# Regrouping the sixteen pairs of a Strassen-type product: four groups of four, with a split first group

## The chip, the cores and the metric

The kernel runs on one core of one Trainium2 chip. The metric is the device time of one execution, in microseconds (us). A core has TensorE (PE in the profile, PEld for its weight loads), VectorE (DVE), ScalarE (ACT), GpSimd (POOL) and SyncE (SP), whose queue issues all the DMA transfers of the part that is changed here.

## The reference

One layer of a streaming encoder on x of shape 1024 x 1024, in float32: a token-mixer sub-layer and then a channel mixer. Only the second half of the channel mixer is touched:

```
h2 = modulate(rms_norm(x, g_pre_mlp), sh2, sc2)
f  = square(relu(h2 @ w_mlp_in))            # 1024 x 4096, the first mixer product
ff = f @ w_mlp_out                          # 4096 -> 1024, the second mixer product
x  = x + gt2 * rms_norm(ff, g_post_mlp)
```

## The kernel before

**Precision.** Every float32 operand is split into a high and a low fp32r part (`split`: a ScalarE cast, line 104, and a VectorE subtraction, line 91), and each product is three matmuls: high by high, high by low, low by high.

**The second mixer product.** The 4096 summed rows are 16 pairs of 128-row slices. For a group of pairs the 2x2 block product is done in seven multiplications instead of eight, in the order 1, 2, 6, 5, 7, 3, 4 (`ORDER`, `STEPS`). A *step* is one of the seven for one group: for each of four row blocks b, one PSUM bank gets three matmuls of 128x512 from every pair of the group (`product`, line 1379), and then the bank is added into the result `acc` in SBUF (`gather`): by a ScalarE copy the first time a quarter of the result is touched (line 1387), by a VectorE addition otherwise (line 1389). The bank family "a" is kept through steps 1, 6, 7 and 4 of a group, "b" serves step 2, "c" steps 5 and 3. PSUM has eight banks here, all in one pool.

**Factors.** A step's left and right factors are raw rows or sums of raw rows. `load` brings the raw rows by roles A, B, C and D (sides x: `w_mlp_out`, y: the stored activation `f_d`), one 256 KB transfer per role, pair and side. `make(n)` adds or subtracts them as `SUMS` says (line 1288), splits the result into `factor_at` tiles, and starts loads for the next group. Pairs 0 and 1 of a group have their raw rows in `g` tiles, pairs 2 and 3 in `h` tiles; the role X (first written in step 2) lives in `wh` and `wl` tiles, two buffers each, which the first mixer product also uses for its outgoing rows (`fo`, stored to `f_d` by line 1340). Factor tiles alternate between two sets (`n % 2`).

**Groups before.** `GROUPS = (2, 4, 4, 4, 2)`. The first group of two pairs starts inside the tail of the first mixer product (`mlp_tail`). The last group of two goes block by block: for one row block all seven steps, then the next block, so that `finish_half` can begin early. `finish_half(b, q)` squares one half of a result block on ScalarE into a scratch tile with a row sum (line 1429), multiplies the half by a gain on VectorE (1432), and, when both halves of the block are in, forms the reciprocal root (129 on VectorE, 132 on GpSimd), adds the residual in two VectorE instructions (1437) and stores (1440).

**Order.** In this part no order is written out by hand. A planner places the instructions on each engine from its own simulated timeline; the program order is a preference, and a tile that has no free buffer makes its first writer wait until an older tile of its tag is released. What is placed first on an engine then runs first.

Of the kernel before, what the change touches and what calls it, by code (L numbers as in the profile page):

```python
# [16 lines left out]
P = 128  # L17
# [13 lines left out]
def block_kernel(  # L31
# [28 lines left out]
    def nm(s):  # L60
        uid[0] += 1
        return f"{s}_{uid[0]}"
# [982 lines left out]
    def gslot(dtype=F32, shape=(P, HALF)):  # L1045
        return gp.tile(list(shape), dtype, tag="g", name=nm("g"))
# [58 lines left out]
    def hslot(dtype=F32, shape=(P, HALF)):  # L1105
        return tk.tile(list(shape), dtype, tag="h", name=nm("h"), bufs=16)
# [132 lines left out]

    GROUPS = (2, 4, 4, 4, 2)
    NG = len(GROUPS)
    HERE = {
        "x": {"A": (0, 0), "B": (0, 1), "C": (1, 1), "D": (1, 0)},
# [13 lines left out]
    raw_at, made_at, made = {}, {}, {}  # L1259
    steps = [(g, i) for g in range(NG) for i in ORDER]  # L1260

    def raw_of(role, j, side):
        if (role, j, side) not in raw_at:
            if role == "X":
                for q in range(2):
                    t = raw_tile((P, 2, HALF), "wh" if side == "x" else "wl")
                    for r in range(2):
                        raw_at["X", 2 * q + r, side] = t[:, r, :]
            else:
                raw_at[role, j, side] = gslot() if j < 2 else hslot()  # L1270
        return raw_at[role, j, side]

    def load(g, role, sides="xy"):
        p0 = sum(GROUPS[:g])
        for j in range(GROUPS[g]):
            for side in sides:
                a, n = HERE[side][role]
                m = 2 * (p0 + j) + a
                src = f_d[m] if side == "y" else w_mlp_out[m * P : (m + 1) * P, :]
                nc.sync.dma_start(raw_of(role, j, side), src[:, halves[n]])  # L1280

    def make(n):

        g, i = steps[n]
        for j in range(GROUPS[g]):
            for side, o, a, b, op in SUMS.get(i, ()):
                o, a, b = (raw_of(r, j, side) for r in (o, a, b))
                nc.vector.tensor_tensor(o, a, b, op=op)
        made[n] = []
        for j in range(GROUPS[g]):  # L1290
            fs = []
            for side in "xy":
                to = factor_at(n, j, side)
                split(raw_of(WHERE[side][i], j, side), *to)
                fs.append(to)
            made[n].append(fs)
        if g + 1 < NG:
            for sides, role in {
                5: [("xy", "A")], 7: [("xy", "B")], 3: [("x", "D"), ("y", "C")],
                4: [("x", "C"), ("y", "D")],  # L1300
            }.get(i, ()):
                load(g + 1, role, sides)

    def factor_at(n, j, side):
        g, i = steps[n]
        if g == NG - 1:
            if i in (5, 7):
                return made_at[0, j + 2 * (i == 7), side]
            if i == 4:
                return made_at[1, j, side]  # L1310
            new = {1: lambda: frslot(), 2: lambda: hslot(F32R), 6: lambda: hslot(F32R),
                   3: lambda: gslot(F32R)}[i]
            return new(), new()
        at = n % 2, j, side
        if at not in made_at:
            new = frslot if j >= 2 and n % 2 else yslot
            made_at[at] = new(), new()
        return made_at[at]

    with ExitStack() as es:  # L1320
        def rest_of_h():
            order = """
                53a 50a s50a 51a 52a s51a n0 n1 51b 50b s52a s31 s30 52b 53b s53a 73a 72a 70 s33 s53b 60 s50b s52b s32 71 72b 62 73b s51b 63 61 42 s62 41 s63 s60 40a s42 s71 s61 43 40b s40 s70 s73 s43 s72 s41
            """
            for step in order.split():
                second_half(step)

        def mlp_products(p, xop):
            fo = out_pair()

            def done(r, half, ps, kept):

                o = fo[r][:, half, :]
                if kept is None:
                    nc.scalar.copy(o, ps)
                else:
                    nc.vector.tensor_tensor(o, ps, kept, op=ALU.add)
                nc.vector.scalar_tensor_tensor(o, o, 0.0, o, op0=ALU.max, op1=ALU.mult)
                if (r, half) in ((0, 1), (1, 0)):
                    nc.sync.dma_start(f_d[2 * p + r], flat(fo[r]))  # L1340

            return pair_products(psg, 4, xop, yop, keeper(fo), done, p == 0)

        def mlp_tail(i):
            if i == 1:
                for role in "ADBC":
                    load(0, role)
            elif i == 5:
                make(0)
            elif i == 3:  # L1350
                make(1)

        pipeline(
            NP, mlp_factors, mlp_products, first=(mlp_first, mlp_split), tail=mlp_tail,
            early=rest_of_h
        )
# [3 lines left out]
    with ExitStack() as es:  # L1360
# [4 lines left out]
        def frslot():  # L1365
            return fr.tile([P, HALF], F32R, tag="fr", name=nm("fr"))
# [5 lines left out]
            (4, "a", False, 0, 1),  # L1372
        )

        def product(ps, fs, b, start):
            s = slice(b * P, (b + 1) * P)
            for j, ((xh, xl), (yh, yl)) in enumerate(fs):
                for n, (l, r) in enumerate(((yh, xh), (yh, xl), (yl, xh))):
                    nc.tensor.matmul(  # L1379
                        ps, l[:, s], r, start=start and j == 0 and n == 0,  # L1380
                        stop=j == len(fs) - 1 and n == 2, skip_group_check=True,
                    )

        def gather(ps, b, half, n, fresh):
            o = acc[:, half * 4 + b, halves[n]]
            if fresh:
                nc.scalar.copy(o, ps)
            else:
                nc.vector.tensor_tensor(o, ps, o, op=ALU.add)  # L1389

        seen = set()
        last = 7 * (NG - 1)
        for n in range(last):
            if n % 7 == 0:
                banks = {}
            i, bk, start, half, c = STEPS[n % 7]
            for b in range(4):
                if start:
                    banks[bk, b] = bank(psg, "s")
                product(banks[bk, b], made[n], b, start)  # L1400
                gather(banks[bk, b], b, half, c, (half, c) not in seen)
            seen.add((half, c))
            for m in {last - 3: (last - 1, last), last - 2: (last + 1, last + 2),
                      last - 1: range(last + 3, last + 7)}.get(n, (n + 2,)):
                make(m)
        g2r = [gslot() for _ in range(2)]
        for q in range(2):
            nc.sync.dma_start(g2r[q], mod_d[3:4, halves[q]].broadcast_to([P, HALF]))

        gpm = raw_tile()  # L1410
        nc.sync.dma_start(gpm, g_post_mlp.broadcast_to([P, D]))
        for q in range(2):
# [4 lines left out]
        def finish_half(b, q):  # L1417

            n, s = halves[q], slice(b * P, (b + 1) * P)
            if b not in blocks:  # L1420
                xt = [fr.tile([P, HALF], F32, tag="fr", name=nm("xt")) for _ in "01"]
                for h in range(2):
                    nc.sync.dma_start(xt[h], x1_d[s, halves[h]])
                blocks[b] = xt, raw_tile(tag="wl" if b < 4 else "wh"), sums()
                again = False
            else:
                again = True
            (xt, sq, ss), o = blocks[b], acc[:, b, n]
            nc.scalar.activation(
                sq[:, n], o, AF.Square, scale=D**-0.5, accum_out=ss[:, q : q + 1]  # L1430
            )
            nc.vector.tensor_tensor(o, o, g2r[q], op=ALU.mult)
            if again:
                r = rstd_of(ss)
                for h in range(2):
                    o = acc[:, b, halves[h]]
                    nc.vector.scalar_tensor_tensor(
                        xt[h], o, r, xt[h], op0=ALU.mult, op1=ALU.add
                    )
                    nc.sync.dma_start(out[s, halves[h]], xt[h])  # L1440


        WHOLE = {2: (0, 0), 7: (1, 1), 3: (1, 0), 4: (0, 1)}
        for b in range(4):
            banks = {}
            for n7, (i, bk, start, half, n) in enumerate(STEPS):
                if start:
                    banks[bk] = bank(psg, "s")
                product(banks[bk], made[last + n7], b, start)
                gather(banks[bk], b, half, n, False)  # L1450
                if i in WHOLE:
                    half, q = WHOLE[i]
                    finish_half(4 * half + b, q)
    tk_es.close()
    gp_es.close()
    psg_es.close()
# [29 lines left out]
```

## Time and profile before

| what | value |
|---|---|
| time, median of 3 runs | 1444.85 us (1442.78 to 1446.96) |
| the profiled execution, its own time | 1447.72 us |
| its span, first to last instruction | 1446.0 us |
| TensorE busy in the span | 1375.6 us (95%) |
| VectorE busy | 1075.1 us (74%) |
| ScalarE busy | 653.0 us (45%) |
| mean granted TensorE clock | 0.983 |

Times in rows are us from the start of the span. A row of the timeline merges instructions of one kind; "x3" says how many, and square brackets give the idle time ahead of them and what ended it.

### The profile page before, as it was taken

How to read it: one execution, taken by the hardware profiler on the slowest of the kernel's cores; microseconds unless marked ns; L12 is line 12 of the kernel's file. 1: busy time of each engine (PE TensorE's matmuls, PEld its weight loads, DVE VectorE, ACT ScalarE, POOL GpSimd, SP SyncE). 2: the span in 40 equal slices, each digit the busy share in tenths (PEclk: the TensorE clock that was granted, in tenths of full speed). 3: DMA queues.
4: the chain of work that ended last, by engine and by line, in shares of the span. 5: the costliest groups of instructions: out<-in, count | busy, mean ns of one | idle time of the engine just before them, and what ended most of it. 6: DMA issues, size and time to landing. Idle time of an engine off the chain costs nothing.

```text
span 1446.0 us, 17935 instructions
## 1 busy us (share of the span) xinstructions
PE 1375.6 (95%) x6281; PEld 1124.2 (78%) x6281; DVE 1075.1 (74%) x1684; ACT 653.0 (45%) x1317; POOL 95.3 (7%) x187
## 2 busy tenths in 40 slices
PE   5899899999999999989999899999999899999996
PEld 4788777887888888767788688888888688888884
DVE  6727887887876878728626976665645999989998
ACT  5636656665534444324446643332332534334432
POOL 1003112211200000000001000000000000000001
PEclk9899999999999999999999899999999999999999
DMA  8501111111124776758423143332336425151224
GB/s 300 181 15 34 37 40 35 37 37 52 45 87 142 248 260 205 221 202 309 146 99 116 45 146 117 117 116 86 113 123 218 153 80 175 59 171 33 81 80 174
DMA packets 111742, 178.43 MB, mean 123 GB/s; under 512 B 7786, under 2 KB 67230, under 8 KB 111652
## 3 DMA queue, kind: packets, MB, share of 16 engines
q1 hardware_dynamic: 111652, 177.29, 37.0%
q8 instruction: 49, 0.80, 0.2%
q14 instruction: 41, 0.34, 0.1%
HBM read 135.83 MB, written 41.43 MB: 123 GB/s over the span
## 4 chain that ended last, share of the span: by engine, by line
PE 69%; DVE 14%; DMA 7%; issue 4%; ACT 3%; POOL 1%; SPq 0%; DVEq 0%; ACTq 0%; POOLq 0%
PE s L234 24%; PE s L1379 19%; PE mm L546 10%; PE v L508 3%; PE s L903 3%; DVE pt L690 2%; PE s L123 2%; PE s L121 2%; PE s L122 2%; DMA wa<-in_w_ada_dram 2%; PE o L731 2%; DVE a L694 2%; PE tr L720 1%; DVE acc L145 1%; DMA raw<-in_w_in_dram 1%
## 5 line engine op out<-in xcount | busy, mean ns | idle before, releaser
L1379 PE MATMUL s<-y,y 128*128 128x512 f32 x984 | 236.7, 393 | 7.9 <-DVE ffacc L1389 4.3
L1379 PEld LDWEIGHTS s<-y,y 128*128 128x128 f32 x984 | 185.3, 189 | 50.0 <-DVE ffacc L1389 5.8
L546 PE MATMUL mm<-hTh,wh 128*128 128x512 f32 x320 | 129.1, 403 | 0.0
L546 PE MATMUL mm<-hTh,wl 128*128 128x512 f32 x320 | 125.5, 392 | 0.0
L546 PE MATMUL mm<-hTl,wh 128*128 128x512 f32 x320 | 125.5, 392 | 0.0
L104 ACT CAST y<-g 128x512 fp32r<-128x512 f32 x104 | 58.8, 622 | 127.1 <-PE s L1379 100.8
L690 DVE TENSOR_TENSOR_SCAN pt<-pt,dmask 128x128 f32<-128x128 f32 (+3 forms) x64 | 87.1, 1365 | 8.7 <-ACT pt L683 8.2
L1389 DVE TENSOR_TENSOR ffacc<-s,ffacc 128x512 f32<-128x512 f32 x124 | 84.2, 696 | 8.1 <-PE s L1379 8.1
L234 PE MATMUL s<-mTh,g 128*128 128x512 f32 x256 | 86.3, 404 | 3.7 <-ACT mTh L104 3.7
L104 ACT CAST tu<-tr 128x512 fp32r<-128x512 f32 (+2 forms) x112 | 49.1, 439 | 78.2 <-PE tr L720 49.4
L132 POOL TENSOR_TENSOR rstd<-var,mhalf 128x1 f32<-128x1 f32 x32 | 23.2, 726 | 879.7 <-DVE var L129 879.5
L91 DVE TENSOR_TENSOR tu<-tr,tu 128x512 fp32r<-128x512 f32 (+2 forms) x112 | 55.1, 494 | 34.5 <-ACT tu L104 33.4
L234 PE MATMUL s<-mTh,h 128*128 128x512 f32 x240 | 79.8, 396 | 0.0
L1379 PE MATMUL s<-fr,fr 128*128 128x512 f32 x288 | 74.5, 392 | 0.0
L234 PE MATMUL s<-y,h 128*128 128x512 f32 x288 | 71.7, 391 | 0.0
L91 DVE TENSOR_TENSOR y<-g,y 128x512 fp32r<-128x512 f32 x104 | 68.6, 697 | 4.0 <-PE s L1379 2.3
L234 PE MATMUL s<-y,g 128*128 128x512 f32 x288 | 71.5, 391 | 0.0
L546 PEld LDWEIGHTS mm<-hTh,wl 128*128 128x128 f32 x320 | 60.2, 188 | 13.4
L234 PE MATMUL s<-hTh,t 128*128 128x512 f32 x208 | 67.5, 394 | 0.0
L546 PEld LDWEIGHTS mm<-hTl,wh 128*128 128x128 f32 x320 | 60.5, 189 | 8.8
L546 PEld LDWEIGHTS mm<-hTh,wh 128*128 128x128 f32 x320 | 60.4, 189 | 8.8
L731 PE MATMUL o<-tu,vs 128*128 128x256 f32 x320 | 57.0, 297 | 9.6 <-DVE ot L741 5.0
(293 smaller groups left out, 3147.7 us busy)
## 6 DMA issues: line engine op xcount, KB each, us to landing
raw<-in_w_in_dram SPq DMA_DIRECT2D x38, 512.0 KB, 5.2
wa<-in_w_ada_dram SPq DMA_DIRECT2D x32, 512.0 KB, 4.3
raw<-in_w_mlp_in_dram SPq DMA_DIRECT2D x32, 512.0 KB, 3.7
g<-in_w_mlp_out_dram SPq DMA_DIRECT2D x40, 256.0 KB, 3.1
g<-f_d SPq DMA_DIRECT2D x40, 256.0 KB, 2.8
f_d<-wl SPq DMA_DIRECT2D x16, 512.0 KB, 4.7
f_d<-wh SPq DMA_DIRECT2D x16, 512.0 KB, 3.2
h<-in_w_mlp_out_dram SPq DMA_DIRECT2D x24, 256.0 KB
```

The source lines that it names most:

```text
L91: eng.tensor_tensor(o, a, b, op=ALU.subtract)
L104: nc.scalar.copy(hi, src)
L121: nc.tensor.matmul(ps, lh, rh, start=i == 0, stop=False)
L122: nc.tensor.matmul(ps, lh, rl, start=False, stop=False)
L234: nc.tensor.matmul(ps, l, r, start=first and k == 0 and j == 0, stop=k == nk - 1 and j == 2, skip_group_check=True,)
L508: nc.tensor.matmul(vb[b], l, r, start=k == 0 and i == 0, stop=k == KC - 1 and i == 2, skip_group_check=True,)
L546: nc.tensor.matmul(ps, w[a][:, k, :], hT[b][:, k, s], start=k == 0 and i == 0, stop=k == KC - 1 and i == 2, skip_group_check=True,)
L690: nc.vector.tensor_tensor_scan(pt[:, 0:w][:, ::-1], pt[:, 0:w][:, ::-1], dmask[:, T - w : T][:, ::-1], 1.0, ALU.mult, ALU.max,)
L731: nc.tensor.matmul(po[:, : 2 * P], v, part[:, 0:5:4, :] if j and jp == g else part[:, 2 * j + 1 : 2 * j + 3, :], start=jp == 0 and j == 0 ...
L903: nc.tensor.matmul(ps, l[:, k, s], r, start=k == 0 and i == 0, stop=k == 3 and i == 2, skip_group_check=True,)
L1379: nc.tensor.matmul(ps, l[:, s], r, start=start and j == 0 and n == 0, stop=j == len(fs) - 1 and n == 2, skip_group_check=True,)
L1389: nc.vector.tensor_tensor(o, ps, o, op=ALU.add)
```

## The change

The 16 pairs are now four groups of four. The two pairs that the first group used to have are the first half of a group of four: steps 1 and 2 are done with pairs 0 and 1 and not gathered, pairs 2 and 3 are loaded and split, and steps 1 and 2 are completed with them and gathered. There is no special last group: the last two steps (3 and 4) of the last group alternate by row block. The halves of blocks that are whole earlier are finished after steps 6 (blocks 0 to 3, first half) and 7 (blocks 4 to 7, second half) of the last group. The scratch tile of `finish_half` is now a `raw` tile (three buffers) for all eight blocks, where it was `wl` for blocks 0 to 3 and `wh` for 4 to 7 (two buffers each); the residual rows of blocks 0 to 3 are loaded into `g` tiles.

```
-    GROUPS = (2, 4, 4, 4, 2)
+    GROUPS = (4, 4, 4, 4)
...
+    FIRST_TWO, LAST_TWO = (0, 1), (2, 3)
...
             if i == 1:
                 for role in "ADBC":
-                    load(0, role)
+                    load(0, role, js=FIRST_TWO)
             elif i == 5:
-                make(0)
+                make(0, FIRST_TWO)
             elif i == 3:
-                make(1)
+                make(1, FIRST_TWO)
...
+        def step(n, blocks=range(4), js=range(4), last=True):
             i, bk, start, half, c = STEPS[n % 7]
-            for b in range(4):
-                if start:
+            fs = [made[n][j] for j in js]
+            for b in blocks:
+                if start and js[0] == 0:
                     banks[bk, b] = bank(psg, "s")
-                product(banks[bk, b], made[n], b, start)
-                gather(banks[bk, b], b, half, c, (half, c) not in seen)
+                product(banks[bk, b], fs, b, start and js[0] == 0, last)
+                if last:
+                    gather(banks[bk, b], b, half, c, (half, c) not in seen)
...
+        step(0, js=FIRST_TWO, last=False)
+        for role in "ADBC":
+            load(0, role, js=LAST_TWO)
+        step(1, js=FIRST_TWO, last=False)
+        for n in range(2):
+            make(n, LAST_TWO)
+        for n in range(2):
+            step(n, js=LAST_TWO)
+            make(n + 2)
+        NS = 7 * NG
+        for n in range(2, NS - 5):
+            step(n)
+            make(n + 2)
...
-            if b not in blocks:
-                xt = [fr.tile([P, HALF], F32, tag="fr", name=nm("xt")) for _ in "01"]
+            again = b in blocks
+            if not again:
+                xt = [gslot() if b < 4 else fr.tile([P, HALF], F32, tag="fr", name=nm("xt")) for _ in "01"]
...
-                blocks[b] = xt, raw_tile(tag="wl" if b < 4 else "wh"), sums()
+                blocks[b] = xt, raw_tile(), sums()
...
-        WHOLE = {2: (0, 0), 7: (1, 1), 3: (1, 0), 4: (0, 1)}
+        for n in range(NS - 5, NS - 2):
+            step(n)
+            if n + 2 < NS:
+                make(n + 2)
+            if n == NS - 5:
+                for b in range(4):
+                    finish_half(b, 0)
+            if n == NS - 3:
+                for b in range(4):
+                    finish_half(4 + b, 1)
         for b in range(4):
-            banks = {}
-            for n7, (i, bk, start, half, n) in enumerate(STEPS):
-                ...
+            step(NS - 2, (b,))
+            finish_half(4 + b, 0)
+            step(NS - 1, (b,))
+            finish_half(b, 1)
```

The branch of `factor_at` that gave the last group of two its own factor tiles is gone.

## Rows read from the trace of the kernel before

**Rows 1.** The page's first part: busy time, share of the span, instructions.
```profile
PE 1375.6 (95%) x6281; PEld 1124.2 (78%) x6281; DVE 1075.1 (74%) x1684; ACT 653.0 (45%) x1317; POOL 95.3 (7%) x187
```
**Rows 2.** Windows of the second product: length, busy time (count) by engine, PE clock, DMA.
```profile
1133.60:1137.10 3.50, 1.73 (x6) 0.86 (x5) 3.50 (x7) 2.59 (x6) 0.00 (x0) 1.00 0.37 150
1137.10:1149.30 12.20, 12.10 (x45) 9.51 (x45) 12.20 (x22) 6.12 (x12) 0.00 (x0) 0.86 0.36 108
1149.30:1151.60 2.30, 0.00 (x0) 0.00 (x0) 2.30 (x5) 0.18 (x1) 0.00 (x0) 1.00 0.40 128
...
1230.00:1390.00 160.00, 160.00 (x702) 131.46 (x701) 150.49 (x250) 67.68 (x126) 0.00 (x0) 1.00 0.25 79
...
1415.00:1428.00 13.00, 11.59 (x51) 9.22 (x50) 12.80 (x25) 5.39 (x17) 1.93 (x3) 1.00 0.70 242
1428.00:1436.20 8.20, 4.97 (x18) 3.14 (x18) 8.20 (x17) 1.89 (x5) 2.00 (x3) 1.00 0.49 180
1436.20:1446.00 9.80, 0.00 (x0) 0.00 (x0) 6.22 (x12) 1.01 (x4) 1.59 (x2) 0.76 0.43 161
```
**Rows 3.** Groups by line and shape, 1122.1 us to the end, VectorE.
```profile
L1389 DVE TENSOR_TENSOR ffacc<-s,ffacc 128x512 f32<-128x512 f32 x124 | 84.2, 696 | 8.1 <-PE s L1379 8.1
```
**Rows 4.** Timeline of all engines, 1100 to 1180 us.
```profile
1111.14 5.60 PE L1379 MATMUL s<-y,y 128*128 128x512 f32 x24
...
1113.56 1.29 DVE L1288 TENSOR_TENSOR wh<-g,g 128x512 f32<-128x512 f32 x2 [1.77 <-DMA f_d<-wh]
...
1122.12 11.52 PE L1379 MATMUL s<-y,y 128*128 128x512 f32 x50
...
1125.12 0.62 ACT L1335 COPY wl<-s 128x512 f32<-128x512 f32 x1
...
1127.40 0.70 DVE L1337 TENSOR_TENSOR wh<-s,wh 128x512 f32<-128x512 f32 x1
...
1133.40 0.70 DVE L1338 SCALAR_TENSOR_TENSOR wh<-wh 128x512 f32<-128x512 f32 x1
...
1134.13 0.32 SPq L1340 DMA_DIRECT2D f_d<-wh  x1
...
1134.27 0.50 PE L1379 MATMUL s<-y,y 128*128 128x512 f32 x1 [0.63 <-ACT ffacc L1387]
...
1135.36 1.19 PE L1379 MATMUL s<-y,y 128*128 128x512 f32 x4 [0.60 <-DVE ffacc L1389]
...
1137.17 12.10 PE L1379 MATMUL s<-y,y 128*128 128x512 f32 x45 [0.61 <-DVE y L91]
...
1138.21 1.31 DVE L1288 TENSOR_TENSOR wl<-h,h 128x512 f32<-128x512 f32 x2
...
1151.61 18.22 PE L1379 MATMUL s<-y,y 128*128 128x512 f32 x78 [2.34 <-DVE y L91]
```
**Rows 5.** SyncE's queue, 1085 to 1130 us: the first and the last loads of h tiles.
```profile
1085.69 0.33 SPq L1280 DMA_DIRECT2D h<-in_w_mlp_out_dram  x1
...
1122.29 0.85 SPq L1280 DMA_DIRECT2D h<-f_d  x2
```
**Rows 6.** Timeline of all engines, 1385 us to the end.
```profile
1434.51 1.66 PE L1379 MATMUL s<-y,y 128*128 128x512 f32 x6 [1.59 <-DVE ffacc L1389]
...
1437.55 0.70 DVE L1389 TENSOR_TENSOR ffacc<-s,ffacc 128x512 f32<-128x512 f32 x1
...
1438.28 0.63 ACT L1429 ACTIVATE wl<-ffacc 128x512 f32<-128x512 f32 x1 [1.80 <-DVE ffacc L1389]
...
1438.75 0.17 DVE L129 SCALAR_TENSOR_TENSOR var<-ss 128x1 f32<-128x1 f32 x1
1438.82 0.19 ACT L1429 ACTIVATION_READ_ACCUMULATOR wl<-ffacc 128x1 f32 x1
...
1439.06 1.59 POOL L132 TENSOR_TENSOR rstd<-var,mhalf 128x1 f32<-128x1 f32 x2 [3.25 <-DVE var L129]
...
1440.17 2.74 DVE L1437 SCALAR_TENSOR_TENSOR xt<-ffacc,rstd,xt 128x512 f32<-128x512 f32 x4 [0.37 <-POOL rstd L132]
```

More of the change, by code (lines that the diff above doesn't have):

```diff
@@ L1271, in raw_of, with load @@
         return raw_at[role, j, side]
-    def load(g, role, sides="xy"):
+    def load(g, role, sides="xy", js=range(4)):
         p0 = sum(GROUPS[:g])
-        for j in range(GROUPS[g]):
+        for j in js:
             for side in sides:
@@ L1280, in load, with make @@
                 nc.sync.dma_start(raw_of(role, j, side), src[:, halves[n]])
-    def make(n):
+    def make(n, js=range(4)):
         g, i = steps[n]
-        for j in range(GROUPS[g]):
+        for j in js:
             for side, o, a, b, op in SUMS.get(i, ()):
@@ L1288, in make @@
                 nc.vector.tensor_tensor(o, a, b, op=op)
-        made[n] = []
-        for j in range(GROUPS[g]):
+        for j in js:
             fs = []
@@ L1295, in make @@
                 fs.append(to)
-            made[n].append(fs)
+            made.setdefault(n, []).append(fs)
         if g + 1 < NG:
@@ L1304, in factor_at @@
     def factor_at(n, j, side):
[L1305 to L1313, printed above, removed]
         at = n % 2, j, side
@@ L1373, in block_kernel, with product @@
         )
-        def product(ps, fs, b, start):
+        def product(ps, fs, b, start, stop=True):
             s = slice(b * P, (b + 1) * P)
@@ L1380, in product @@
                         ps, l[:, s], r, start=start and j == 0 and n == 0,
-                        stop=j == len(fs) - 1 and n == 2, skip_group_check=True,
+                        stop=stop and j == len(fs) - 1 and n == 2, skip_group_check=True,
                     )
@@ L1389, in gather @@
                 nc.vector.tensor_tensor(o, ps, o, op=ALU.add)
[L1391 to L1394, printed above, removed]
-                banks = {}
+        seen, banks = set(), {}
+        def step(n, blocks=range(4), js=range(4), last=True):
             i, bk, start, half, c = STEPS[n % 7]
-            for b in range(4):
-                if start:
+            fs = [made[n][j] for j in js]
+            for b in blocks:
+                if start and js[0] == 0:
                     banks[bk, b] = bank(psg, "s")
-                product(banks[bk, b], made[n], b, start)
-                gather(banks[bk, b], b, half, c, (half, c) not in seen)
[L1402 to L1405, printed above, removed]
+                product(banks[bk, b], fs, b, start and js[0] == 0, last)
+                if last:
+                    gather(banks[bk, b], b, half, c, (half, c) not in seen)
+            if last and blocks[-1] == 3:
+                seen.add((half, c))
+        step(0, js=FIRST_TWO, last=False)
[11 more added lines that the diff above has]
+            make(n + 2)
         g2r = [gslot() for _ in range(2)]
@@ L1419, in finish_half @@
             n, s = halves[q], slice(b * P, (b + 1) * P)
-            if b not in blocks:
-                xt = [fr.tile([P, HALF], F32, tag="fr", name=nm("xt")) for _ in "01"]
+            again = b in blocks
+            if not again:
+                xt = [gslot() if b < 4 else fr.tile([P, HALF], F32, tag="fr", name=nm("xt")) for _ in "01"]
                 for h in range(2):
                     nc.sync.dma_start(xt[h], x1_d[s, halves[h]])
-                blocks[b] = xt, raw_tile(tag="wl" if b < 4 else "wh"), sums()
-                again = False
-            else:
-                again = True
+                blocks[b] = xt, raw_tile(), sums()
             (xt, sq, ss), o = blocks[b], acc[:, b, n]
@@ L1440, in finish_half @@
                     nc.sync.dma_start(out[s, halves[h]], xt[h])
-        WHOLE = {2: (0, 0), 7: (1, 1), 3: (1, 0), 4: (0, 1)}
-        for b in range(4):
-            banks = {}
-            for n7, (i, bk, start, half, n) in enumerate(STEPS):
[L1447 to L1453, printed above, removed]
+        for n in range(NS - 5, NS - 2):
[8 more added lines that the diff above has]
+                    finish_half(4 + b, 1)
+        for b in range(4):
+            step(NS - 2, (b,))
+            finish_half(4 + b, 0)
+            step(NS - 1, (b,))
+            finish_half(b, 1)
     tk_es.close()
```

## Prediction

> **What bounds the kernel now.** I read the page first: TensorE is busy for 95% of the span [rows 1]. Then I cut the second mixer product into windows, because an average hides where the rest is. From 1230 to 1390 us TensorE never idles: 702 matmuls in 160 us, 0.228 us each [rows 2]. There the kernel is TensorE's, and a saving on VectorE (150.5 us busy of 160) is worth nothing. The loss sits at the two ends. From 1122.12 us on, with one step of 24 matmuls already done [rows 4], 1344 - 24 = 1320 matmuls remain (16 pairs x 7 steps x 4 blocks x 3 = 1344). At 0.228 us they would end at 1423.1. The last one ends at 1434.51 + 1.66 = 1436.2 [rows 6]: 13.1 us are lost. Of these I can place:
> - at the start 1.8 + 0.1 + 2.3 us idle (window minus TensorE busy), and 45 matmuls in 12.10 us at a granted clock of 0.86, 0.269 us each: 45 x 0.041 = 1.8. Together 6.0 [rows 2];
> - in the last group 1.4 + 3.2 = 4.6 us idle [rows 2];
> - 2.5 us that no row places alone: slower spacing in the last group and the rounding of the rate.
>
> Both ends have VectorE busy without a break [rows 2]. After the last matmul come 9.8 us of VectorE work and stores.
>
> **The change, part by part.**
>
> *Matmuls:* none added or removed.
>
> *Gathers.* Five groups of 28 become four: 140 to 112, and the 16 ScalarE copies stay, so VectorE's 124 [rows 3] become 96. Two VectorE instructions take 1.31 us where one takes 0.70 [rows 4], so 0.60 us apart: 28 x 0.60 = 16.8 us of VectorE time less. This pays only where VectorE held TensorE, at the two ends. Sums and splits go by pairs and stay the same number.
>
> *The start.* In VectorE instructions from 1113.56 us, where its unbroken work begins: 11 left from the first product and step 2 of the first two pairs; steps 1 and 2 of the other pairs, 4 + 8; step 6, 12 sums and 8 splits. That is 43, ending at 1113.56 + 43 x 0.60 = 1139.4, or 1141.8 with four gathers of step 2 in between. TensorE from 1122.12 has step 2 of the first half and both steps of the second half, 72 x 0.228 = 16.4 us, so it wants step 6 at 1138.5: it waits 0.9 to 3.3 us. Step 5 (16 more instructions) is ready at 1151.4 and wanted at 1149.5; step 7 at 1158.6, wanted at 1160.5: VectorE has caught up. Sums that are placed ahead of need lengthen this. Before, the same count in program order gives no wait of a microsecond, yet 6.0 us were lost, so order costs. Bounds: 0.9 (ideal order) and 9 (3.3 plus the whole 6.0 of before). I take 4.0, nearer to the counted wait, with some loss of clock in it.
>
> *What X waits for.* The X tiles of pairs 2 and 3 reuse `wh` and `wl`, which hold the first product's last rows until they are stored: the last store is issued at 1134.13 and the first such sum runs at 1138.21 [rows 4]. Before, these sums belonged to a later group; now they stand ahead of step 6 of the first. From then 4 X sums and 10 further instructions, 8.4 us, plus a cast of 0.6, give 1147.2. TensorE can fill 1138.5 to 1144.0 with step 6 of pairs 0 and 1 (24 matmuls, 5.5 us), and begins pair 2 before pair 3 is ready. This stays inside the 4.0.
>
> *The 16 loads for pairs 2 and 3.* The same h tiles were loaded at 1085.69 to 1122.29 before [rows 5], well ahead of their place in the program, since only tiles released by the first product hold them. I cost them at nothing: they are needed from 1127 on. If the last landed as late as the store-to-sum distance above (4.1 us), that is 1127.2, still before step 2's second half at 1133. The queue behind them holds nothing else urgent.
>
> *The end.* The last group no longer does 28 gathers of two-pair products, so TensorE's 4.6 us there should go. Step 4's factors can be cast only when step 7's last matmuls release the tile set; 8 casts and 8 subtractions, some 5.5 us, against 2.7 us of step 3's first block, but three other blocks of step 3 can be taken first. I take 0.7, bounds 0 and 2.8 (5.5 - 2.7). Of the 2.5 unplaced I keep 0.5. Last matmul: 1423.1 + 4.0 + 0.7 + 0.5 = 1428.3, against 1436.2.
>
> *Scratch tiles.* Here the change adds a wait. A scratch tile is held from the first to the second half of a block. After step 6 blocks 0 to 3 ask for one each, and there are three; each goes back only after that block's step 4. Block 3 and blocks 4 to 7 wait. Let T be the start of step 3's first block; TensorE needs 96 x 0.228 = 21.9 us from there. Block 0 is whole at T + 5.5 and its tile goes to block 3, which keeps it to the end. Block 1 is whole at T + 10.9; its tile then passes through blocks 4, 5, 6 and 7. So VectorE, with little to do until T + 11.1, has after that 5 gathers and 11 gain products (16 x 0.60 = 9.6 us), 14 residual additions (four in 2.74 us [rows 6]: 9.6) and 7 small sums of at most 0.17 (1.2): 20.4 us, to T + 31.5. The stores end 3.1 us after the last addition (1442.9 to 1446.0) [rows 6], so T + 34.6: 12.7 us after the last matmul, where it was 9.8. Lower bound with nothing queued: gather 0.7, square and read 0.8, product 0.6, small sum and root about 1.0 (two roots in 1.59), two additions 1.4, store 3.1, together 7.6. Upper bound: blocks 4 to 7 and 3 all after the last matmul, a gather and 9 products (6.0), 10 additions (6.9), 5 small sums (0.9), the first square and root (1.8), store 3.1: 18.7. I take 12.7, since TensorE's own pace brings block 1 whole long before the end. On ScalarE a waiting square can have only other squares behind it: step 4's 8 casts must stand ahead, or block 0 would never give its tile back.
>
> *Residual rows in g tiles* need releases of the last group's raw rows, which step 7's and step 3's splits give long before a residual addition: nothing, or one landing (4.1 at most) if that cover were gone.
>
> **Sum.** 1428.3 + 12.7 = 1441.0 against a span of 1446.0: 5.0 us less. The profiled execution took 1447.72 us, 1.7 outside the span and 0.2% above the median of the runs. From the median: 1444.85 - 5.0 = 1439.9 us. A measurement of this kernel can tell some 0.3%, 4.3 us, from no change.
>
> **Rivals.**
> - *The scratch tiles do not queue* (the planner passes them on earlier, or VectorE's order suits it): a tail of 7.6 to 9.8, so 1434.8 to 1437.0. For it: the order is the planner's. Against: three tiles for four open blocks.
> - *The start loses as much as before or more, through PSUM.* Steps 1 and 2 of the first half hold all eight banks from their first matmul to the gathers of the second half. At 1122 two banks still belong to the first product and are released by line 1335 at 1125.7 and 1337 at 1128.1 [rows 4]; two blocks last until 1124.9. If the second half of step 1 is not placed between, TensorE idles 3.2 us, and at the clock seen after such a gap loses 1.8 more: 1444.9, no change. For it: two of the four early gaps were ended by gathers (0.63 and 0.60 us). Against: the largest (2.34) and one of 0.61 were ended by factor splits [rows 4]. The Trainium skill, "Perfetto Trace Analysis", Optimization Strategy, says that a gap repeating on the engine that should be saturated can mean too little SBUF or PSUM for the next tile. By that rule this rival's 1444.9 would be the forecast; by the rows, which give most of the idle time to VectorE's splits, 1439.9; the trace agrees with the rule in part.
> - *Slower: X of pairs 2 and 3.* VectorE ran line 1337 at 1127.40 and the dependent 1338 six us later [rows 4]; if the planner lets more of the now larger pile of sums ahead of it, the store and X slip. To be slower by 4.3 us than before, the start must lose 4.0 + 5.0 + 4.3 = 13.3, so X must begin about 9 to 12 us after 1138.2, some 15 to 20 instructions later. 1449 to 1452. Against: the store came before X with a similar pile.
>
> **How the numbers follow.** Forecast 0.45, own range 1437 to 1443, a little over half of it beyond 0.3%; no queue 0.22; PSUM 0.18; slower 0.15. Faster 0.25 + 0.22 = 0.47; same 0.20 + 0.18 = 0.38 (which takes in the slower part of the forecast); slower 0.15. The range 1434.5 to 1447.5 takes in the first three and leaves out the slower rival and the lowest corner, some 2 in 10.
>
> **What would show it.** 96 gathers of line 1389. Last matmul near 1428, no idle TensorE between 1160 and step 3 of the last group. TensorE's idle at 1138 to 1152 under 4 us. Squares (line 1429) of blocks 3 to 7 standing behind step 4's blocks 0 and 1, and 12 to 13 us after the last matmul. Wrong would be a last matmul after 1433, or a first X sum of pairs 2 and 3 after 1145.

## The result and the profile after

The changed kernel took 1437.17 us (median of 6 runs, 1433.91 to 1439.89) against 1445.98 us for the kernel before beside it (median of 6, 1442.78 to 1447.57). The ratio is 0.9946, with a 95% interval of 0.9932 to 0.9960: 7.8 us less (5.8 to 9.8). The forecast was 1439.9 us and 5.0 us less: the direction and the range hold, the size was too small.

The profiled executions show where: the span went from 1446.0 to 1437.7 us. It is best cut at two marks, TensorE's first and last matmul of the second mixer product.

| stretch | before | after | difference | forecast |
|---|---|---|---|---|
| start of the span to the first matmul of the second product | 1111.1 | 1109.1 | -2.1 | 0 |
| first to last matmul of the second product | 325.0 | 314.3 | -10.7 | -7.9 |
| last matmul to the end of the span (the tail) | 9.8 | 14.3 | +4.5 | +2.9 |
| sum | 1446.0 | 1437.7 | -8.3 | -5.0 |

The first line is not the change's. TensorE's instructions ahead of that mark are the same in both kernels, and in the profiled executions of all the kernels below the mark lies anywhere from 1105.4 to 1111.4 us. The 2.1 us arise within the first 55 us: the last eight matmuls of line 461, far ahead of the code that was changed, start at 54.22 us before and at 51.39 after, and in two executions of one and the same kernel (scratch per half, below) at 49.99 and 54.39. So below, the two lower lines are what is compared.

First the windows of the second product, all engines (length, busy time and count of PE, PEld, DVE, ACT and POOL, granted clock, DMA share and GB/s), to be held against [rows 2]:

```profile
1120.06:1133.90 13.84, 13.84 (x62) 11.38 (x61) 13.84 (x24) 6.97 (x15) 0.00 (x0) 1.00 0.84 284
1133.90:1137.20 3.30, 3.30 (x16) 2.70 (x15) 0.05 (x1) 0.53 (x2) 0.00 (x0) 1.00 0.97 387
1137.20:1148.40 11.20, 11.20 (x50) 9.01 (x48) 11.16 (x19) 6.58 (x12) 0.00 (x0) 1.00 0.05 15
1148.40:1150.00 1.60, 0.13 (x1) 0.00 (x0) 1.60 (x4) 1.24 (x3) 0.00 (x0) 1.00 0.66 205
1150.00:1160.00 10.00, 9.99 (x44) 8.27 (x45) 10.00 (x17) 5.46 (x10) 0.00 (x0) 1.00 0.71 234
...
1230.00:1390.00 160.00, 160.00 (x702) 131.60 (x701) 147.28 (x242) 63.55 (x122) 0.00 (x0) 1.00 0.31 99
1390.00:1401.50 11.50, 11.50 (x51) 9.39 (x51) 8.00 (x14) 4.78 (x10) 0.00 (x0) 1.00 0.13 46
1401.50:1411.30 9.80, 9.80 (x44) 8.05 (x43) 5.82 (x10) 1.97 (x4) 0.00 (x0) 1.00 0.01 2
1411.30:1423.40 12.10, 12.10 (x53) 9.59 (x52) 11.05 (x23) 7.65 (x22) 4.00 (x5) 1.00 0.20 75
1423.40:1437.70 14.30, 0.01 (x1) 0.00 (x0) 11.22 (x21) 1.45 (x4) 3.52 (x4) 0.67 0.62 230
```

One gap of 1.48 us is all that is left of 8.8 us of idle time, the clock stays at 1.00 up to the last matmul, and the middle has the same 702 matmuls in 160 us as before. The seven waits of before are one. The timeline of TensorE shows it, with the gap in brackets:

```profile
1109.08 5.60 PE L1371 MATMUL s<-y,y 128*128 128x512 f32 x24
...
1120.06 7.90 PE L1371 MATMUL s<-y,y 128*128 128x512 f32 x34
...
1150.01 4.82 PE L1371 MATMUL s<-fr,fr 128*128 128x512 f32 x20 [1.48 <-DVE fr L91]
```

The gap stands ahead of step 5's matmuls with pairs 2 and 3: in the first group only steps 2, 5 and 3 keep factors in `fr` tiles, for these two pairs, and step 2 is done with them by 1136.7. The split that ends it is the low part of an X factor of step 5. The two ScalarE casts of this kind were over by 1145.6, and VectorE came to the first of their subtractions 3.7 us later, after six other instructions (rows of ScalarE, then VectorE):

```profile
1144.95 0.62 ACT L104 CAST fr<-wh 128x512 fp32r<-128x512 f32 x1
```

```profile
1149.27 0.69 DVE L91 TENSOR_TENSOR fr<-wh,fr 128x512 fp32r<-128x512 f32 x1
```

From 1120.06 us the 1320 matmuls that remain would take 301.0 us at 0.228 each and end at 1421.1. The last ended at 1423.4: 2.3 us lost, where it was 13.1. VectorE's gathers are 96, as worked out (groups by line and shape over the whole span):

```profile
L1381 DVE TENSOR_TENSOR ffacc<-s,ffacc 128x512 f32<-128x512 f32 x96 | 65.5, 691 | 16.9 <-PE s L1371 16.9
```

The tail got longer. The squares of `finish_half` on ScalarE, from the timeline of ACT between 1340 us and the end; the other 12 are left out:

```profile
1368.88 0.63 ACT L1435 ACTIVATE raw<-ffacc 128x512 f32<-128x512 f32 x1
...
1370.54 0.63 ACT L1435 ACTIVATE raw<-ffacc 128x512 f32<-128x512 f32 x1
...
1371.68 0.63 ACT L1435 ACTIVATE raw<-ffacc 128x512 f32<-128x512 f32 x1
...
1411.36 0.64 ACT L1435 ACTIVATE raw<-ffacc 128x512 f32<-128x512 f32 x1 [7.88 <-DVE ffacc L1381]
```

Three squares run, one for each scratch tile, then none for 39 us, though the halves of block 3 and (after step 7) of blocks 4 to 7 are whole. The fourth square in this list opens the rest: 13 squares, and with them most of VectorE's finishing, come after 1411 us. The start of step 3, the gather that makes block 0 whole, the last matmuls, the last residual additions and the last stores, from the timeline of all engines:

```profile
1401.29 6.76 PE L1371 MATMUL s<-y,y 128*128 128x512 f32 x29
...
1410.63 0.69 DVE L1381 TENSOR_TENSOR ffacc<-s,ffacc 128x512 f32<-128x512 f32 x1 [1.39 <-PE s L1371]
...
1421.86 1.55 PE L1371 MATMUL s<-fr,fr 128*128 128x512 f32 x6
...
1433.21 1.41 DVE L1443 SCALAR_TENSOR_TENSOR g<-ffacc,rstd,g 128x512 f32<-128x512 f32 x2
1433.98 1.00 SPq L1446 DMA_DIRECT2D out_dram<-g  x2
```

VectorE works until 1434.6 us, 11.2 us after the last matmul; the stores take the remaining 3.1 us.

### The profile page after: what moved, and what is told of

Its sections match the earlier page's. It is cut to its first block, busy times and chain, and to the rows that moved or that the text cites. A ratio compares the mean times of both kernels' runs of the same rounds, so it can differ in the third digit from the quotient of the medians.

```text
span 1437.7 us, 17905 instructions
## 1 busy us (share of the span) xinstructions
PE 1368.7 (95%) x6281; PEld 1120.3 (78%) x6281; DVE 1058.7 (74%) x1656; ACT 653.7 (45%) x1317; POOL 97.2 (7%) x187
## 4 chain that ended last, share of the span: by engine, by line
PE 71%; DVE 14%; DMA 6%; issue 4%; ACT 3%; POOL 1%; SPq 0%; DVEq 0%; ACTq 0%; POOLq 0%
PE s L234 26%; PE s L1371 18%; PE mm L546 10%; PE s L903 3%; PE v L508 3%; DVE pt L690 2%; PE s L122 2%; PE s L123 2%; PE s L121 2%; PE o L731 2%; DMA raw<-in_w_in_dram 2%; DVE a L694 2%; DMA wa<-in_w_ada_dram 2%; PE tr L720 1%; POOL a L686 1%
## 5 line engine op out<-in xcount | busy, mean ns | idle before, releaser
L1371 PE MATMUL s<-y,y 128*128 128x512 f32 x1008 | 239.6, 390 | 0.0
L1371 PEld LDWEIGHTS s<-y,y 128*128 128x128 f32 x1008 | 189.3, 188 | 40.4
L104 ACT CAST y<-g 128x512 fp32r<-128x512 f32 x96 | 53.5, 620 | 114.7 <-PE s L1371 97.0
L1371 PE MATMUL s<-fr,fr 128*128 128x512 f32 x336 | 87.1, 392 | 1.5 <-DVE fr L91 1.5
L1381 DVE TENSOR_TENSOR ffacc<-s,ffacc 128x512 f32<-128x512 f32 x96 | 65.5, 691 | 16.9 <-PE s L1371 16.9
L1371 PEld LDWEIGHTS s<-fr,fr 128*128 128x128 f32 x336 | 63.0, 188 | 16.0 <-DVE fr L91 1.9
```

The lines of the kernel that those rows point to most:

```text
L104: nc.scalar.copy(hi, src)
L1371: nc.tensor.matmul(ps, l[:, s], r, start=start and j == 0 and n == 0, stop=stop and j == len(fs) - 1 and n == 2, skip_group_check=True,)
```

## Experiments

Each time is the median of the runs made beside the kernel before, with the ratio and its 95% interval. "Product" is the stretch from the first to the last matmul of the second product and "tail" the rest of the span, both from the run's profiled execution. Diffs are against the changed kernel. Kernels whose start is that of the changed one idle 0.5 to 1.6 us at the gap ahead of step 5, two executions of one kernel 0.6 and 1.6, so differences of 1 us in the last column say nothing.

| kernel | time, us | ratio (interval) | product, us | tail, us | TensorE idle in the product, us |
|---|---|---|---|---|---|
| before | 1445.98 | 1 | 325.0 | 9.8 | 8.8 |
| changed | 1437.17 | 0.9946 (0.9932 to 0.9960) | 314.3 | 14.3 | 1.5 |
| changed, again | 1439.87 | 0.9953 (0.9937 to 0.9969) | 314.0 | 14.3 | 1.2 |
| scratch per half | 1432.63 | 0.9906 (0.9890 to 0.9923) | 314.4 | 10.4 | 1.6 |
| scratch per half, again | 1433.10 | 0.9915 (0.9900 to 0.9930) | 313.5 | 10.4 | 0.6 |
| row sums only | 1438.54 | 0.9947 (0.9932 to 0.9963) | 313.7 | 14.3 | 0.8 |
| start unsplit | 1435.74 | 0.9942 (0.9921 to 0.9962) | 313.0 | 14.3 | 0.2 |
| X in raw tiles | 1439.44 | 0.9956 (0.9943 to 0.9969) | 313.9 | 14.2 | 0.8 |
| scratch per half, X in raw | 1433.44 | 0.9920 (0.9907 to 0.9933) | 313.9 | 10.5 | 0.8 |
| scratch per half, start unsplit | 1434.41 | 0.9921 (0.9904 to 0.9938) | 313.3 | 10.4 | 0.5 |
| 28 more on VectorE, second group | 1442.73 | 0.9984 (0.9972 to 0.9996) | 318.4 | 14.3 | 3.7 |
| 16 more on VectorE, spread | 1439.53 | 0.9959 (0.9947 to 0.9972) | 314.0 | 14.3 | 0.5 |
| 16 more on VectorE, first group | 1449.20 | 1.0030 (1.0018 to 1.0042) | 323.1 | 15.3 | 7.9 |
| last group in two | 1453.10 | 1.0054 (1.0036 to 1.0073) | 320.9 | 23.7 | 4.9 |

**The changed kernel again**, as the yardstick.

> The changed kernel itself once more, as the yardstick for the other kernels of this group on the same chip. Both theories: a ratio to the kernel before of 0.993 to 0.996, and a tail of 13.5 to 15 us from the last matmul to the end of the span.

As expected: 0.9953, tail 14.3 us.

**Scratch tiles per half, against the row sums.** The scratch tile only takes the output of the square that nobody reads, so it need not be kept between a block's halves. The row sums, which must be kept, had six buffers for eight blocks; eight column pairs of a constant tile whose contents are spent take their place, alone in the second kernel:

```
-                blocks[b] = xt, raw_tile(), sums()
-            (xt, sq, ss), o = blocks[b], acc[:, b, n]
+                blocks[b] = xt, vec[:, 2 * b : 2 * b + 2]
+            (xt, ss), sq, o = blocks[b], raw_tile(), acc[:, b, n]
...
(row sums only)
+                blocks[b] = xt, raw_tile(), vec[:, 2 * b : 2 * b + 2]
```

> Each half of a block gets a scratch tile of its own, which goes back right after the square; the row sums move to eight spare columns of a constant tile. Theory (held scratch tiles pile the finishing work up behind block 0): the squares of block 3 and blocks 4 to 7 run as soon as their halves are whole, the tail after the last matmul falls from 14.3 us to 8 to 10, and the time by 4 to 6 us against the changed kernel, a ratio to the kernel before of 0.990 to 0.992. Rival (the tail is VectorE's own work, whatever waits): the tail stays above 12.5 us and the ratio at 0.994 to 0.996.

> Only the row sums move (they had six buffers for eight blocks); the scratch tiles are held as in the changed kernel. Theory of the scratch tiles: no change, tail 13.5 to 15 us, ratio 0.993 to 0.996. Rival (the six row-sum tiles are the queue): the tail falls to 8 to 10 us with this alone.

> Scratch tiles per half once more, on the chip of this group, for comparison: ratio 0.989 to 0.992, tail 10 to 11 us.

The row sums alone change nothing (tail 14.3). With scratch tiles per half the tail is 10.4 us, 3.9 less, in both executions, a little above the 8 to 10 expected of the first; the product is as it was within 0.8 us. The timeline of the first one shows squares and residual additions standing among step 3 and step 4, and the first block stored 14 us before the last matmul ends (all engines, rows between left out):

```profile
1402.89 0.63 ACT L1435 ACTIVATE raw<-ffacc 128x512 f32<-128x512 f32 x1 [1.34 <-DVE ffacc L1381]
...
1405.40 1.42 DVE L1443 SCALAR_TENSOR_TENSOR xt<-ffacc,rstd,xt 128x512 f32<-128x512 f32 x2
...
1406.18 1.00 SPq L1446 DMA_DIRECT2D out_dram<-xt  x2
...
1418.66 1.55 PE L1371 MATMUL s<-fr,fr 128*128 128x512 f32 x6
...
1426.19 1.41 DVE L1443 SCALAR_TENSOR_TENSOR g<-ffacc,rstd,g 128x512 f32<-128x512 f32 x2 [0.73 <-POOL rstd L132]
```

So the held scratch tiles were the queue, and they cost 3.9 us of the change's gain. This version beats both kernels: 0.9906 and 0.9915, 12.3 us less than before by the second of them (10.1 to 14.5). Beside the changed kernel of its own group of runs the first is 7.2 us faster, more than the 4 to 6 expected and than the 3.9 of the profiles; each ratio is good for about 2.3 us either way, and the lead-in varies besides, so the two do not contradict each other. The 3.9 us, which both executions show, are the safer number.

**The start, unsplit.** The steps of the first group are written whole; the second halves of their factors are made first:

```
-        step(0, js=FIRST_TWO, last=False)
         for role in "ADBC":
             load(0, role, js=LAST_TWO)
-        step(1, js=FIRST_TWO, last=False)
         for n in range(2):
             make(n, LAST_TWO)
         for n in range(2):
-            step(n, js=LAST_TWO)
+            step(n)
             make(n + 2)
```

> The four pairs of the first group are taken at once: steps 1 and 2 are written as whole steps, and the second halves of their factors are made ahead of them. Theory A (the split in the program is what saves the start): TensorE idles 3 to 6 us between 1115 and 1140 us, and the ratio to the kernel before is 0.997 to 0.999. Theory B (the planner starts with the pairs that are ready anyway, and what saves the start is less VectorE work per matmul): idle time and ratio as in the changed kernel within 1.5 us, 0.993 to 0.996.

Theory B. The planner takes the 24 matmuls of step 1 with the first two pairs ahead of the end of the first product all the same, and the gap ahead of step 5 is not larger, 0.17 us (timeline of TensorE):

```profile
1106.51 5.60 PE L1371 MATMUL s<-y,y 128*128 128x512 f32 x24
...
1146.12 4.81 PE L1371 MATMUL s<-fr,fr 128*128 128x512 f32 x20 [0.17 <-DVE fr L91]
```

What helps the start is therefore not how the split is written. Together with scratch tiles per half it adds nothing that can be measured:

> Scratch tiles per half and the first group's steps written whole. Each alone gave its part without harm, so together: as with scratch tiles per half alone within 1.5 us, ratio 0.989 to 0.992, tail 9.5 to 11 us. If the unsplit form gains a little by itself (1 us of TensorE idle time less), 0.0005 lower than the other.

Ratio 0.9921, as the scratch tiles alone within the intervals.

**X of pairs 2 and 3 without the wait.**

```
-                    t = raw_tile((P, 2, HALF), "wh" if side == "x" else "wl")
+                    t = raw_tile((P, 2, HALF), "raw" if q else "wh" if side == "x" else "wl")
```

> The X tiles of pairs 2 and 3 come from the raw tiles, which are free long before the first product's last rows are stored. Theory (X waits for that store): VectorE's 3.3 us of idle time near 1134 us and TensorE's 1.5 us near 1148 go; 1 to 2.5 us less than the changed kernel up to the last matmul. But two of the three raw tiles are then held into the last group, so the scratch tiles come later and the tail may grow by 0 to 3 us. Rival (the sums before step 6 bound the start whatever X does): TensorE still idles 1 to 2 us there.

> Scratch tiles per half and X of pairs 2 and 3 in raw tiles together. If both theories hold the gains add: a ratio to the kernel before of 0.988 to 0.991, no TensorE idle time after 1120 us, a tail of 8 to 10 us. If X is not what TensorE waits for: as with scratch tiles per half alone, 0.990 to 0.992.

In the changed kernel VectorE stands idle for 3.3 us until the store of `wl` has landed (first row). Here the first X sum of these pairs runs some 7 us earlier and VectorE does not idle there (second row, first product 2.3 us later in this execution), yet TensorE still waits (third row):

```profile
1137.24 1.29 DVE L1290 TENSOR_TENSOR wl<-h,h 128x512 f32<-128x512 f32 x2 [3.29 <-DMA f_d<-wl]
```

```profile
1130.34 0.68 DVE L1290 TENSOR_TENSOR raw<-h,h 128x512 f32<-128x512 f32 x1
...
1145.28 2.60 PE L1371 MATMUL s<-y,y 128*128 128x512 f32 x10 [0.84 <-ACT y L104]
```

The product is 313.9 us against 314.0: nothing gained. The rival holds, with 0.8 us of idle time where it gave 1 to 2: the wait for X is real, and what TensorE waits for afterwards comes late without it too. Nor did the kernel with both edits gain over scratch tiles alone (0.9920).

**VectorE work put back, in three places.** A subtraction that makes a low part is done twice, which adds work to VectorE alone; the planner then places everything anew. The comments say which kernel has which line:

```
                 split(raw_of(WHERE[side][i], j, side), *to)
+                if side == "x" and 9 <= n < 16:                # 28, second group
+                if side == "x" and n in (2, 3, 4, 5):          # 16, first group
+                if side == "x" and j == 0 and 7 <= n < 23:     # 16, spread
+                    sub(to[1], raw_of(WHERE[side][i], j, side), f(to[0]), nc.vector)
```

> 28 subtractions on VectorE are done twice, four in each of seven steps of the second group (16.8 us of VectorE time, as much as the gathers that the change removed), with the same results. Theory (TensorE bounds the middle): no change against the changed kernel within 1.5 us, ratio 0.993 to 0.996. Rival (what counts is VectorE's total): up to 16.8 us more, ratio 1.000 to 1.006.

> 16 subtractions on VectorE are done twice, four each in steps 6, 5, 7 and 3 of the first group (9.6 us), with the same results. Theory (VectorE's work per matmul is what lost the start before): TensorE's idle time in the first group grows from 1.5 to 4 to 8 us, 3 to 7 us more than the changed kernel, ratio 0.9965 to 0.9995. Rival (order or PSUM banks lost it): less than 1.5 us more, 0.993 to 0.996.

> 16 subtractions on VectorE are done twice, one in each of 16 steps of the second, third and fourth group (9.6 us, as many as were added to the first group alone before), with the same results. Theory (only a stretch in which VectorE's work exceeds TensorE's costs time): 0.6 us more per step of 10.9 us fits into VectorE's slack there, so no change against the changed kernel within 1.5 us from TensorE's first to its last matmul of the second product (314 us), ratio 0.993 to 0.996. Rival (VectorE's total counts): 5 to 10 us more, 0.998 to 1.002.

The first missed: 4.4 us more (318.4 against 314.0), neither nothing nor 16.8. The size was badly chosen. Seven steps take TensorE 336 x 0.228 = 76.6 us, and VectorE has (88 + 28) x 0.60 = 69.6 us of its own in them; 16.8 more overfill the stretch. Its windows show VectorE full and TensorE waiting just there:

```profile
1250.00:1275.00 25.00, 25.00 (x111) 20.59 (x110) 25.00 (x43) 8.00 (x14) 0.00 (x0) 1.00 0.19 63
...
1290.00:1300.00 10.00, 7.19 (x25) 5.83 (x26) 10.00 (x18) 2.08 (x4) 0.00 (x0) 0.83 0.35 101
```

With 9.6 us spread over 16 steps the slack takes it all: 314.0, no change. The same 9.6 us in the first group cost 9.0 (323.1), more than the 3 to 7 expected, and the ratio, 1.0030, is above the range given. Windows of that kernel from the gap on:

```profile
1145.00:1154.00 9.00, 1.11 (x4) 0.68 (x3) 9.00 (x16) 1.67 (x4) 0.00 (x0) 0.68 0.57 186
1154.00:1165.00 11.00, 11.00 (x40) 8.60 (x40) 11.00 (x20) 4.75 (x9) 0.00 (x0) 0.79 0.41 123
```

The gap alone is 7.9 us; after it 40 matmuls take 11.0 us at a granted clock of 0.79, 0.275 each: 1.9 more. VectorE is full throughout the gap, but its work is not all that changed. The gap ends with a cast of a sum of step 6 for pairs 2 and 3 (rows of VectorE, then TensorE):

```profile
1152.13 0.68 DVE L1290 TENSOR_TENSOR h<-wh,h 128x512 f32<-128x512 f32 x1
```

```profile
1153.51 2.08 PE L1373 MATMUL s<-y,y 128*128 128x512 f32 x4 [7.89 <-ACT y L104]
```

Counted from the first matmul of the product, this sum runs at 45.9 us. In the changed kernel it runs at 43.8, only 2.1 earlier: nine more VectorE instructions stand ahead of it (5.4 us), some added and some moved, but VectorE's wait for the store is almost gone (0.2 us where it was 3.3). What differs is that the changed kernel has 20 matmuls of step 5 with pairs 2 and 3 ahead of those that need this sum. So the run shows that the start has no room for this work; how much of the 9.0 us is the work and how much the other order was not separated.

**Five groups with the new order of the end.** `make`, `load` and `step` take the pairs of their group, and

```
-    GROUPS = (4, 4, 4, 4)
+    GROUPS = (4, 4, 4, 2, 2)
```

> Groups of 4, 4, 4, 2 and 2 pairs with the changed kernel's start and its order of the end: five groups again, so 28 VectorE gathers more than the changed kernel, all in the last quarter of the product, but not the old order block by block. Theory (at the end too VectorE's work per matmul lost the time): TensorE idles 4 to 10 us in the last 76 us before the last matmul, ratio 0.997 to 1.002. Rival (the old order block by block, with six matmuls to a bank, lost it): TensorE idles less than 1.5 us there, ratio 0.993 to 0.996.

The product takes 6.8 us more than the changed kernel's. TensorE idles 3.6 us in the last 76 (1.3 more at the start), each time until VectorE has made a split or a gather, and 68 matmuls at a granted clock of 0.91 take 0.266 us each, 2.6 more. The idle time is a little under the 4 to 10 expected and well over the rival's 1.5. The ratio, 1.0054, is above the range given, because the tail becomes 23.7 us, which was not expected. Its windows:

```profile
1375.00:1400.00 25.00, 23.18 (x103) 18.86 (x101) 25.00 (x43) 11.08 (x20) 0.00 (x0) 1.00 0.23 72
1400.00:1420.00 20.00, 18.10 (x68) 13.69 (x69) 19.02 (x32) 6.31 (x14) 0.00 (x0) 0.91 0.38 119
...
1440.00:1456.00 16.00, 0.00 (x0) 0.00 (x0) 12.39 (x23) 0.00 (x0) 4.76 (x6) 0.50 0.71 262
```

The 9.4 us that the tail is longer are not shown to be the gathers'. The scratch tiles queue here too, and longer: the third square is followed by none for 23 us, and the fourth runs 0.6 us before the last matmul ends, so that 13 of the 16 halves are squared from then on (timeline of ScalarE):

```profile
1407.65 0.64 ACT L1437 ACTIVATE raw<-ffacc 128x512 f32<-128x512 f32 x1 [3.03 <-DVE g L1423]
...
1431.26 0.63 ACT L1437 ACTIVATE raw<-ffacc 128x512 f32<-128x512 f32 x1 [4.55 <-DVE ffacc L1382]
```

Five groups with scratch tiles per half, which would tell the two apart, were not run.

## Why the prediction came out as it did

- *The middle is TensorE's; the two ends are VectorE's.* Right for the middle: 9.6 us of VectorE work spread over it cost nothing. Borne out at the ends: in the first group the same work cost 9.0 us, in part perhaps through the order, and with groups of two at the end, 28 gathers more, the product took 6.8 us longer, with every wait of TensorE there ended by VectorE.
- *96 gathers, worth something only at the ends.* The count is right; what they are worth by place is shown by the same runs, as far as these go.
- *The start, 4.0 us.* Mis-sized, and the main miss. The prediction counted a wait of 0.9 to 3.3 us ahead of step 6 and added a share for sums placed out of order and for a lower clock. TensorE did not wait for step 6 at all: the planner made the sums of step 6 for the first two pairs early and ran step 5 ahead of the rest of step 6. The one gap, 1.48 and 1.17 us in the two profiled executions of the changed kernel, came ahead of step 5, whose factors the prediction's count had ready 1.9 us after they were wanted (1151.4 against 1149.5). So the size lay inside the counted range, but not at the counted place, and the clock did not fall. The start has little to spare all the same: that is what the 16 subtractions in it showed.
- *The end, 0.7 us and 0.5 unplaced.* TensorE has no idle time there: VectorE is idle for 3.5 of 11.5 and 4.0 of 9.8 us just ahead of the end. Together with the start, 2.3 us lost against the 5.2 forecast, 1.5 of them the gap and 0.8 placed by no row: this term is 2.9 us of the miss in the forecast's favour.
- *The scratch tiles queue.* Right in mechanism and shown by removing it, with the row sums ruled out. The size was short: a tail of 14.3 where 12.7 was worked out. What was off is the time at which block 0 gives back its tile. The prediction had block 0 whole after 24 matmuls, 5.5 us after the start of step 3. Step 3 starts at 1401.29, the gather that makes block 0 whole runs at 1410.63, after 40 matmuls, and the square that opens the queue at 1411.36, 10.1 us in: the planner ran block 1's step 3 and a part of its step 4 among block 0's matmuls. The prediction itself names such an order for TensorE and did not carry it over to the scratch tiles. So at 11.1 us, where it has VectorE begin with 11 gain products, 14 residual additions and 7 small sums, the rows still hold 12, 16 and 8. At the prediction's prices that is 2.1 us more, against the 1.6 by which the tail is longer.
- *X waits for a store.* The wait is there (3.3 us of VectorE), a cost on TensorE was not found: without the wait the product is no shorter. The slower rival built on it did not come: the first X sum ran at 1137.2, not after 1145.
- *PSUM holds up the start.* Did not come: no gap between 1120 and 1148 us. By the Trainium skill, "Perfetto Trace Analysis", Optimization Strategy, a repeated gap can mean too little buffer space for the next tile. At TensorE's one gap that was not what decided here, since a split ended it; at the tail, where five whole halves (block 3 and blocks 4 to 7) waited for a scratch tile with the rest behind them, it was, though the gap there is on ScalarE and VectorE, not on the engine that should be saturated.
- *The total.* The two misses have opposite signs: 2.8 us more gained in the product than forecast, 1.6 lost again in the tail. That the time came within 3 us of the forecast owes something to this luck. By the two lower stretches alone the change is worth 6.2 us. The remaining 2.1 us of the profiled difference lie ahead of the changed code, in executions whose lead-in varies by 6 us; why it varies is open.

## What to carry to other kernels

Count an engine's spare time by stretch: the same 9.6 us of VectorE work was free in one part of this product and went with 9.0 us more in another. When a loop is reordered so that several units of work are open at once, look at every buffer that is held from a unit's first part to its last, above all one whose contents nobody reads: here a tile that could have gone back at once held up most of the finishing work and cost 3.9 us. Where a planner sets the order, an added instruction can move others too: look at what the engine waits for before putting a cost down to the work alone. What a planner can reorder by itself (the split start) need not be written into the program.

## What was not expected of the hardware

A gap of 1.48 us left TensorE's granted clock at 1.00, its upper level, in the window after it (1150 to 1160 us). The gap of 7.9 us was followed by 11 us at 0.79. Before the change, three gaps of 0.6 us each, 1.77 us of idle time in 3.5, were followed by 12.2 us at 0.86 [rows 2]; both values are means that lie between the upper level and the lower one, 0.50 (the last window of the kernel with five groups). The gap of 2.3 us right after that was followed by 78 matmuls in 18.22 us, 0.234 each [rows 4], and a window of that stretch has the clock at 1.00 again:

```profile
1151.60:1160.00 8.40, 8.39 (x37) 6.92 (x38) 8.40 (x15) 2.38 (x5) 0.00 (x0) 1.00 0.56 183
```

The length of a gap alone does not tell here whether the clock falls.
